# Single PSUM banks in the RG and SSD stages of a hybrid decoder layer on one Trainium2 core

## The chip, the core and the metric

The kernel runs on one core of a Trainium2 chip. The core has five engines that work side by side, each through its own instructions in their order: TensorE (PE) multiplies matrices, VectorE (DVE) and ScalarE (ACT) work elementwise, GpSimd (POOL) does some of that and issues transfers, SyncE (SP) issues transfers. TensorE writes its results to PSUM, which here is used as eight banks of 512 fp32 columns for each of the 128 partitions; VectorE and ScalarE read them there. Everything else lies in SBUF, and transfers (DMA) bring data from and to the memory outside. Engines wait for one another by semaphores.

The metric is the time of one execution in microseconds of device time. An interval or a difference of about 0.2% can be told from noise when several runs are made.

## The reference

One layer of a decoder for 512 prompt tokens and 32 sample tokens, 544 in all, with model width 1024, in fp32:

```python
def layer(x, pos, rg_h0, rg_buf, ssd_h0, ssd_buf, p):
    x = x + 0.5 * rmsnorm(swiglu(rmsnorm(x, p['n_ffn1_pre']), ...), p['n_ffn1_post'])
    mix, new = mixer(rmsnorm(x, p['n_mix_pre']), pos, rg_h0, rg_buf, ssd_h0, ssd_buf, p)
    x = x + rmsnorm(mix, p['n_mix_post'])
    x = x + 0.5 * rmsnorm(swiglu(rmsnorm(x, p['n_ffn2_pre']), ...), p['n_ffn2_post'])
    return x, new

def mixer(u, pos, rg_h0, rg_buf, ssd_h0, ssd_buf, p):
    proj = u @ p['w_in']
    rg_x, rg_g, z, xbc, dt_raw, g_rg, g_ssd = jnp.split(proj, cuts, axis=-1)
    rg_xc, rg_buf_new = causal_conv(rg_x, rg_buf, p['rg_conv_w'], p['rg_conv_b'])
    h, rg_h_new = rg_lru(rg_xc, pos, rg_h0, ...)
    y_rg = h * jax.nn.gelu(rg_g)
    xbc_c, ssd_buf_new = causal_conv(xbc, ssd_buf, p['ssd_conv_w'], p['ssd_conv_b'])
    xs, Bs, Cs = jnp.split(jax.nn.silu(xbc_c), ...)
    y, ssd_h_new = ssd_scan(xh, dt, A, Bs, Cs, ssd_h0)
    y = (y + p['ssd_d'][:, None] * xh) * jax.nn.silu(z)
    y_ssd = y * lax.rsqrt(jnp.mean(y * y, per group) + EPS) * p['ssd_norm_w']
    m = (jax.nn.sigmoid(g_rg) * (y_rg @ p['w_proj_rg'])
         + jax.nn.sigmoid(g_ssd) * (y_ssd @ p['w_proj_ssd']))
    return m @ p['w_out'], new
```

`ssd_scan` goes through each of 8 groups of 4 heads in chunks of 128 tokens, with a state from chunk to chunk; the 8 sample sequences of 4 tokens start from stored states.

## The kernel before

The activations stand transposed: features on partitions, the 544 tokens along the free dimension, in two halves of TH = 272. Every fp32 operand of a large product is split into a high and a low part (`xh`, `xl`; `wh`, `wl`), and a product is the sum of high x high, low x high and high x low, in a fast fp32 format. A **unit** is one 128-column block of weights against all tokens: 8 feature blocks k x 3 passes x 2 halves = 48 matmuls of 128 x 272. `W.get()` hands out the next split weight block and lets later ones be loaded (SP) and split (ScalarE L80, VectorE L83), four blocks deep.

The order of TensorE's instructions is the program's order. On the other engines a scheduler orders them by priority, by default that of the program; `urgent()` raises it, weight splits have a lower one.

PSUM is one pool with three kinds of tiles: `acc`, two slots of two banks each, for the large products; `ps`, two slots of one bank, for small products and transposes; `py`, one slot of two banks. A slot is given to the next tile in turn, and that tile's first write waits until the earlier tile in it was read for the last time.

`gemm` (L289) multiplies both halves in turn, k by k, so that the two banks of an `acc` tile are complete at the same time; `unit` calls it. `unit2` (L338) multiplies two weight blocks together with k outermost, so that the operand blocks are released one after the other during the product. `gemm_half` (L327) takes one half alone; the feed-forward stages and the first products of the mixer use it.

In the **RG and SSD stages** the units of `w_in` run in the order of `specs`: the RG inputs and gates in pairs (`rg_inputs`, `rg_gates`), the merge gates (`gate_units`: Tanh on ScalarE, then a transfer to `th_dram`), and for each group g of 8 four convolution inputs (`conv_in`, into a buffer `cb` from `conv_buf`, of which there are 6), for some g two merge gates, and two z units (Tanh and a copy on ScalarE, a product on VectorE, into one of 4 buffers `z`). `t_ahead` counts the buffers `cb` and `z` in use and runs background steps until one is free.

**Background steps** (`bg`) are generators with the small work: `rg_steps`, `conv_steps`, `group_steps`. After every 4th matmul (5th from the last gates on) `ptick` runs one step, so that small products stand between the large ones in TensorE's order. `group_steps` of a group runs `A(c)` for the four chunks (one `ps` tile: L1063 the product C x B, L1065 three transposes; VectorE L1073, L1078 and ScalarE L1081 read it), `Bs(c)` (L1104, L1106 into `py`, L1108 into `ps`), and for the sample tokens `s1` (L1154), `s2` (L1187, two `ps` tiles of transposed states, copied by ScalarE at L1190), `s3` (L1203, L1210) and `s4`. The order on TensorE is A(0), A(1), s1, Bs(0), A(2), s2, s2, Bs(1), A(3), s3 and so on, with 4 to 15 large matmuls between them. Between A and A of two groups some 65 us pass. `scale_state` on GpSimd prepares the state for the next `Bs`.

Then the **projections**: `projected` loads the 8 blocks of `y_rg` (later of `y_ssd`) with `load_split` (SP; ScalarE L251 for `xh`, VectorE L252 for `xl`, in the place of the operands before), multiplies six units and one `unit2`, and each result is merged with its gate by VectorE (L1390; L1393 and L1394). The background steps of the last two groups still run beside them. After `drain()` the second half of the SSD projection follows, whose first unit takes a `py` tile.

Of the kernel before, what the change touches and what calls it, by code (L numbers as in the profile page):

```python
# [18 lines left out]
P = 128  # L19
D = 1024  # L20
KD = 8
# [82 lines left out]
def hybrid_layer_kernel(  # L104
# [21 lines left out]
    psum = ctx.enter_context(tc.tile_pool(name="psum", bufs=1, space=PSUM))  # L126

    def acc_tile():
        return psum.tile([P, 2, 512], F32, tag="acc", name="acc", bufs=2)

    def ps_tile():
        return psum.tile([P, 512], F32, tag="ps", name="ps", bufs=2)

    def py_tile():
        return psum.tile([P, 2, 512], F32, tag="py", name="py", bufs=1)
# [194 lines left out]
    def unit2(kt, rh, rl):  # L330

        wb = [W.get(), W.get()]
        accs = [acc_tile(), acc_tile()]
        for k in range(kt):
            for j in range(2):
                for i, (w, r) in enumerate(((wb[j][0], rh), (wb[j][0], rl), (wb[j][1], rh))):
                    for h in range(2):
                        PE.matmul(accs[j][:, h, :TH], w[:, k, :], r[k][:, HALF[h]],  # L338
                                  start=(k == 0 and i == 0), stop=(k == kt - 1 and i == 2))
                        ptick()  # L340
        return accs
# [256 lines left out]
    banks = []  # L598
    for t in (acc_tile(), acc_tile()):
        banks += [t[:, 0, :], t[:, 1, :]]  # L600
    banks += [ps_tile(), ps_tile()]
    t = py_tile()
    banks += [t[:, 0, :], t[:, 1, :]]
    for k in range(KD):
        to_half(banks[k], [x for x, n in first], [n for x, n in first], k)
    turned = []
    for k in range(KD):
        turned.append(evac_half(banks[k][:, :TH], 0, k))
# [707 lines left out]
    def gate_units(qs, accs=None):  # L1316
        for q in qs:
            for i in range(2):
                acc = accs[i] if accs else unit(KD, xh, xl)
                th = mt([P, T], "th", 2)  # L1320
                S.activation(two(th), acc[:, :, :TH], AF.Tanh, scale=0.5)
                dma(th_dram[2 * q + i], th)
# [5 lines left out]
    S.activation(two(dt_), adt[:32, :, :TH], AF.Identity, bias=dtc[:, 0:1])  # L1328
    bg.append(rg_steps(2, bufs[2:], gsb[2:]))
# [8 lines left out]
    for g in range(8):  # L1338
        out = {}
        for i, f in enumerate((16 + g, 24 + g, 2 * g, 2 * g + 1)):  # L1340
            acc = unit(KD, xh, xl)
# [7 lines left out]
        for i in range(4, 6):  # L1349
            acc = unit(KD, xh, xl)  # L1350
            out[i] = t_ahead("z", NZ)[:, :T]
# [9 lines left out]
    gate_units(GATES_SSD[7][-1:], unit2(KD, xh, xl))  # L1361
# [14 lines left out]
    def projected(src):  # L1376

        ops = [load_split(src[k], k) for k in range(KD)]
        oh, ol = [a[0] for a in ops], [a[1] for a in ops]
        for n in range(KD):  # L1380
            if n < 6:
                acc = unit(KD, oh, ol)
            else:
                if n == 6:
                    accs = unit2(KD, oh, ol)
                acc = accs[n - 6]
            yield n, acc

    for n, acc in projected(yr_dram):
        V.scalar_tensor_tensor(two(yb[:, n, :]), two(gate(n)), 1.0, acc[:, :, :TH], op0=ALU.add, op1=ALU.mult)  # L1390
# [235 lines left out]
```

## Time and profile before

| | us |
|---|---|
| runs (3) | 1742.36, 1743.77, 1746.11 |
| median | 1743.77 |
| the profiled execution | 1742.75 |
| its span, first to last instruction | 1741.0 |
| mean granted TensorE clock | 0.987 of full speed |

The span falls into the first feed-forward stage (to 451 us), first products of the mixer (to 494), RG stage (to some 606), SSD stage with the projections beside its end (to 1213), and then the second half of the SSD projection, the output projection and the second feed-forward stage.

How to read it: a busy time is the union of an engine's instructions; a matmul's end is modelled, and matmuls overlap, so 292 ns for one doesn't mean 292 ns of TensorE. In lists of waits, "PE ps L1063 <- ACT big L1190" says that TensorE's instruction of line 1063, which writes a tile `ps`, stood idle until ScalarE's instruction of line 1190, which writes a tile `big`, was done. In a timeline the first two columns are start and duration in us. PEclk is the share of its full clock that TensorE was granted.

### The profile page before, as it was taken

To read this page: it belongs to the slowest core of one execution; us is meant where nothing else is said; L and a number is where in the kernel's file an instruction comes from. 1 tells how busy PE (TensorE), PEld (TensorE's weight loads), DVE (VectorE), ACT (ScalarE), POOL (GpSimd) and SP (SyncE) were. 2 spreads that over 40 slices of the span, in tenths; PEclk is the share of its full clock that TensorE was granted. 3 is DMA by queue.
4 is the path that set the end of the run, shared out by engine and by line. 5 is a ranking of instruction groups with operands and counts; after the bars stand their busy time and mean duration, and the time that the engine had idled before them with its cause. 6 is when DMAs were issued, how large, how long until landed. Compare 5 with 4: busy or idle time off the path is not lost. (4 is left out here: it accounts for less than half of the span.)

```text
span 1741.0 us, 32086 instructions
## 1 busy us (share of the span) xinstructions
PE 1688.7 (97%) x13479; PEld 1644.9 (94%) x13479; DVE 1002.2 (58%) x1766; ACT 741.4 (43%) x1205; POOL 266.0 (15%) x376
## 2 busy tenths in 40 slices
PE   9999999999999998999999999999999999999997
PEld 7999999999999997998998989989999999999997
DVE  6532333247757578789688787876558322333345
ACT  5323221234568674455445445434246422221233
POOL 0000000000322125335244334230000000000000
PEclk8999999999999998999999999999999999999998
DMA  6213322232543333534453445666333322223231
GB/s 215 97 60 111 97 74 98 87 106 88 185 135 119 94 101 104 164 96 115 141 157 101 134 132 156 213 185 217 130 106 113 116 80 97 97 74 97 85 110 52
DMA packets 205551, 206.21 MB, mean 118 GB/s; under 512 B 10461, under 2 KB 191785, under 8 KB 205150
## 3 DMA queue, kind: packets, MB, share of 16 engines
q1 hardware_dynamic: 196588, 178.49, 32.8%
q0 software_dynamic: 8336, 24.54, 4.3%
q8 instruction: 106, 1.74, 0.4%
q10 hardware_dynamic: 482, 1.12, 0.2%
q14 instruction: 39, 0.32, 0.1%
HBM read 178.43 MB, written 25.69 MB: 117 GB/s over the span
## 5 line engine op out<-in xcount | busy, mean ns | idle before, releaser
L80 ACT CAST wh<-wraw 128x1024 fp32r<-128x1024 f32 (+1 forms) x274 | 283.7, 1037 | 643.0 <-PE acc L289 534.4
L289 PE MATMUL acc<-xh,wh 128*128 128x272 f32 x2576 | 543.6, 292 | 0.1
L289 PE MATMUL acc<-xh,wl 128*128 128x272 f32 x2576 | 540.9, 291 | 0.0
L289 PE MATMUL acc<-xl,wh 128*128 128x272 f32 x2576 | 538.4, 290 | 0.0
L83 DVE TENSOR_TENSOR wl<-wraw,wh 128x1024 fp32r<-128x1024 f32 (+1 forms) x274 | 331.4, 1212 | 318.3 <-ACT wh L80 315.2
L289 PEld LDWEIGHTS acc<-xh,wh 128*128 128x128 f32 x2576 | 408.3, 190 | 3.6 <-issue 1.4
L289 PEld LDWEIGHTS acc<-xh,wl 128*128 128x128 f32 x2576 | 406.4, 190 | 2.6 <-issue 1.2
L289 PEld LDWEIGHTS acc<-xl,wh 128*128 128x128 f32 x2576 | 407.5, 189 | 1.2 <-issue 0.4
L327 PE MATMUL acc<-xh,wh 128*128 128x272 f32 x384 | 114.9, 299 | 0.0
L327 PE MATMUL acc<-xl,wh 128*128 128x272 f32 x384 | 112.1, 292 | 0.0
L327 PE MATMUL acc<-xh,wl 128*128 128x272 f32 x384 | 111.1, 293 | 0.0
L395 DVE TENSOR_TENSOR gate<-gate,acc 128x544 f32<-128x544 f32 x36 | 26.0, 721 | 130.1 <-PE acc L289 130.1
L887 DVE SCALAR_TENSOR_TENSOR cv<-cb,hp,cv 128x568 f32<-128x568 f32 x96 | 93.9, 978 | 1.1
L289 PE MATMUL acc<-hh,wh 128*128 128x272 f32 x448 | 92.5, 288 | 0.0
L289 PE MATMUL acc<-hl,wh 128*128 128x272 f32 x448 | 92.2, 287 | 0.0
L289 PE MATMUL acc<-hh,wl 128*128 128x272 f32 x448 | 92.2, 288 | 0.0
L1576 POOL TENSOR_TENSOR xtok<-xtok,yo 32x512 f32<-32x512 f32 x1 | 1.3, 1256 | 537.8 <-ACT yo L1575 537.8
L747 POOL MEMSET cb<- 128x3 f32 x40 | 4.2, 104 | 505.9 <-PE acc L327 430.9
L327 PE MATMUL acc<-hh,wh 128*128 128x272 f32 x256 | 75.3, 294 | 2.4 <-DVE yb L451 2.4
L327 PE MATMUL acc<-hl,wh 128*128 128x272 f32 x256 | 74.3, 290 | 0.2
L327 PEld LDWEIGHTS acc<-xh,wh 128*128 128x128 f32 x384 | 73.4, 191 | 1.0
L327 PE MATMUL acc<-hh,wl 128*128 128x272 f32 x256 | 74.1, 290 | 0.0
(399 smaller groups left out, 2646.2 us busy)
## 6 DMA issues: line engine op xcount, KB each, us to landing
wraw<-in_w_in_dram SPq DMA_DIRECT2D x34, 1024.0 KB, 5.8
wraw<-in_ffn_wu_dram SPq DMA_DIRECT2D x24, 1024.0 KB, 5.6
wraw<-in_ffn_wg_dram SPq DMA_DIRECT2D x23, 1024.0 KB, 5.1
wraw<-in_ffn_wd_dram SPq DMA_DIRECT2D x20, 1024.0 KB, 5.2
wraw<-in_w_in_dram SPq DMA_DIRECT2D x18, 512.0 KB, 4.2
big<-acs_dram SPq DMA_DIRECT2D x32, 256.0 KB, 5.5
big<-in_state_ssd_dram SPq DMA_DIRECT2D x32, 256.0 KB, 6.0
out_dram<-big POOLq DMA_DIRECT2D x32, 256.0 KB, 3.5
```

Source lines behind the costliest of these rows:

```text
L80: c = nc.scalar.copy(h[:, :kt], src)
L83: nc.vector.tensor_sub(l[:, :kt], src, h[:, :kt].bitcast(F32))
L289: PE.matmul(acc[:, h, :TH], w[:, k, :], r[k][:, HALF[h]], start=(k == 0 and i == 0), stop=(k == kt - 1 and i == 2))
L327: PE.matmul(acc[:, j, :TH], wb[w][:, k, :], r[k][:, HALF[h]], start=(n == 0), stop=(n == len(order) - 1))
L395: V.tensor_mul(two(gs[j]), two(gs[j]), acc[:, :, :TH])
L747: G.memset(buf[:, 0:3], 0.0)
L887: V.scalar_tensor_tensor(o[:, :CO], buf[:, k:k + CO], ws[k], o[:, :CO], op0=ALU.mult, op1=ALU.add)
L1576: G.tensor_add(x[:n, cs], x[:n, cs], o[:n])
```

## The change

From the merge gates of the RG stage to the end of the first half of the SSD projection, PSUM is divided otherwise: `acc` is three slots of one bank, `ps` three slots of one bank, `py` as before. A class `Banks` closes the pool and opens it anew at `banks.open(True)` and, after the `drain()` of the projections, at `banks.open(False)`; a tile of the new pool waits for the readers of the earlier tiles in its bank.

`halves` takes the place of `unit` there: the first half of the tokens is multiplied through all k into one bank and handed to `out`, then the second half into the next bank. `unit2` takes three `acc` banks and one `ps` bank. Evacuations that took both halves in one instruction (gates, RG gates, z, the merges) take two. `conv_buf`, `t_ahead` and the load of a gate tile come ahead of the products whose results go there.

```diff
     def acc_tile():
-        return psum.tile([P, 2, 512], F32, tag="acc", name="acc", bufs=2)
+        assert not banks.single
+        return banks.pool.tile([P, 2, 512], F32, tag="acc", name="acc", bufs=2)
+
+    def bank_tile():
+        assert banks.single
+        return banks.pool.tile([P, 512], F32, tag="acc", name="acc", bufs=3)
 
     def ps_tile():
-        return psum.tile([P, 512], F32, tag="ps", name="ps", bufs=2)
+        return banks.pool.tile([P, 512], F32, tag="ps", name="ps", bufs=3 if banks.single else 2)
...
+    def halves(out):
+        wb = W.get()
+        for h in range(2):
+            a = bank_tile()
+            for k in range(KD):
+                for i, (w, r) in enumerate(((wb[0], xh), (wb[0], xl), (wb[1], xh))):
+                    PE.matmul(a[:, :TH], w[:, k, :], r[k][:, HALF[h]],
+                              start=(k == 0 and i == 0), stop=(k == KD - 1 and i == 2))
+                    ptick()
+            out(a[:, :TH], h)
+
-    def unit2(kt, rh, rl):
+    def unit2(outs):
         wb = [W.get(), W.get()]
-        accs = [acc_tile(), acc_tile()]
-        for k in range(kt):
+        accs = [[bank_tile(), bank_tile()], [bank_tile(), ps_tile()]]
+        for k in range(KD):
             for j in range(2):
...
+        for j in range(2):
+            for h in range(2):
+                outs[j](accs[j][h][:, :TH], h)
...
     def rg_inputs(r):
-        bufs = []
-        for j in range(2):
-            acc = unit(KD, xh, xl)
-            bufs.append(rg_buf(r + j))
-            for h in range(2):
-                conv_in(bufs[j], acc[:, h, :TH], h)
+        bufs = [rg_buf(r), None]
+        halves(lambda a, h: conv_in(bufs[0], a, h))
+        bufs[1] = rg_buf(r + 1)
+        halves(lambda a, h: conv_in(bufs[1], a, h))
         return bufs
...
             g = t_ahead("z", NZ)[:, :T]
-            S.copy(two(g), acc[:, :, :TH])
+            halves(lambda a, h: S.copy(g[:, HALF[h]], a))
...
+    def gate_out(n):
+        th = mt([P, T], "th", 2)
+        def out(a, h):
+            S.activation(th[:, HALF[h]], a, AF.Tanh, scale=0.5)
+            if h == 1:
+                dma(th_dram[n], th)
+        return out
...
+    banks.open(True)
     bg.append(rg_steps(2, bufs[2:], gsb[2:]))
...
         for i, f in enumerate((16 + g, 24 + g, 2 * g, 2 * g + 1)):
-            acc = unit(KD, xh, xl)
             buf = conv_buf(...)
-            for h in range(2):
-                conv_in(buf, acc[:, h, :TH], h)
+            halves(lambda a, h: conv_in(buf, a, h))
...
-            S.activation(two(out[i]), acc[:, :, :TH], AF.Tanh, scale=0.5)
-            S.copy(two(zr), acc[:, :, :TH])
+            def gated(a, h):
+                S.activation(z[:, HALF[h]], a, AF.Tanh, scale=0.5)
+                S.copy(zr[:, HALF[h]], a)
+            halves(gated)
...
+    def projected(src, out_of):
+        for k in range(KD):
+            xh[k], xl[k] = load_split(src[k], k)
+        for n in range(KD - 2):
+            halves(out_of(n))
+        unit2([out_of(n) for n in range(KD - 2, KD)])
+
+    def rg_out(n):
+        t = gate(n)
+        def out(a, h):
+            cs = HALF[h]
+            V.scalar_tensor_tensor(yb[:, n, cs], t[:, cs], 1.0, a, op0=ALU.add, op1=ALU.mult)
+        return out
...
+    projected(yr_dram, rg_out)
+    projected(ys_dram[:KD], ssd_out)
     drain()
+    banks.open(False)
```

`ssd_out` is like `rg_out`, with the product into the gate tile and, after the second half, the addition to `yb`. The rest of the diff gives other names to local lists called `banks`.

More of the change, by code (lines that the diff above doesn't have):

```diff
@@ L125, in hybrid_layer_kernel, with __init__, open, close @@
     dram = ctx.enter_context(tc.tile_pool(name="dram", bufs=1, space=DRAM))
-    psum = ctx.enter_context(tc.tile_pool(name="psum", bufs=1, space=PSUM))
-    def acc_tile():
-        return psum.tile([P, 2, 512], F32, tag="acc", name="acc", bufs=2)
+    class Banks:
+        def __init__(self):
+            self.stack = None
+            self.open(False)
+        def open(self, single):
+            if self.stack is not None:
+                self.stack.close()
+            self.single = single
+            self.stack = ExitStack()
+            self.pool = pool_of(self.stack, "psum", space=PSUM)
+        def close(self):
+            self.stack.close()
+    banks = Banks()
+    def acc_tile():
+        assert not banks.single
[3 more added lines that the diff above has]
+        return banks.pool.tile([P, 512], F32, tag="acc", name="acc", bufs=3)
     def ps_tile():
-        return psum.tile([P, 512], F32, tag="ps", name="ps", bufs=2)
+        return banks.pool.tile([P, 512], F32, tag="ps", name="ps", bufs=3 if banks.single else 2)
     def py_tile():
-        return psum.tile([P, 2, 512], F32, tag="py", name="py", bufs=1)
+        return banks.pool.tile([P, 2, 512], F32, tag="py", name="py", bufs=1)
     FCH = (6, 8, 8)
@@ L1309, in rg_gates, with gate_units @@
         for j in range(2):
-            acc = unit(KD, xh, xl)
             g = t_ahead("z", NZ)[:, :T]
-            S.copy(two(g), acc[:, :, :TH])
+            halves(lambda a, h: S.copy(g[:, HALF[h]], a))
             gsb.append(g)
         return gsb
-    def gate_units(qs, accs=None):
+    def gate_out(n):
[5 more added lines that the diff above has]
+        return out
+    def gate_units(qs):
         for q in qs:
             for i in range(2):
[L1319 to L1322, printed above, removed]
+                halves(gate_out(2 * q + i))
     set_pace(4)
@@ L1349, in hybrid_layer_kernel @@
         for i in range(4, 6):
-            acc = unit(KD, xh, xl)
-            out[i] = t_ahead("z", NZ)[:, :T]
+            z = out[i] = t_ahead("z", NZ)[:, :T]
             zr = mt([P, T], "th", 2)
-            S.activation(two(out[i]), acc[:, :, :TH], AF.Tanh, scale=0.5)
-            S.copy(two(zr), acc[:, :, :TH])
+            def gated(a, h):
+                S.activation(z[:, HALF[h]], a, AF.Tanh, scale=0.5)
+                S.copy(zr[:, HALF[h]], a)
+            halves(gated)
             V.scalar_tensor_tensor(out[i], out[i], 1.0, zr, op0=ALU.add, op1=ALU.mult)
@@ L1360, in hybrid_layer_kernel @@
     gate_units(GATES_SSD[7][:-1])
-    gate_units(GATES_SSD[7][-1:], unit2(KD, xh, xl))
+    unit2([gate_out(2 * GATES_SSD[7][-1] + i) for i in range(2)])
     def load_split(src, k):
@@ L1374, in gate, with ssd_out, out @@
         return t
[L1376 to L1390, printed above, removed]
-    for n, acc in projected(ys_dram[:KD]):
-        t = gate(8 + n)
-        V.scalar_tensor_tensor(two(t), two(t), 1.0, acc[:, :, :TH], op0=ALU.add, op1=ALU.mult)
-        V.tensor_add(yb[:, n, :], yb[:, n, :], t)
+    def projected(src, out_of):
[10 more added lines that the diff above has]
+        return out
+    def ssd_out(n):
+        t = gate(8 + n)
+        def out(a, h):
+            cs = HALF[h]
+            V.scalar_tensor_tensor(t[:, cs], t[:, cs], 1.0, a, op0=ALU.add, op1=ALU.mult)
+            if h == 1:
+                V.tensor_add(yb[:, n, :], yb[:, n, :], t)
+        return out
+    projected(yr_dram, rg_out)
+    projected(ys_dram[:KD], ssd_out)
     drain()
+    banks.open(False)
     ops = [load_split(ys_dram[8 + k], k) for k in range(KD)]
@@ L1586, in hybrid_layer_kernel @@
     drain()
+    banks.close()
     px.close()
```

26 lines of the change are left out of this document (12 added, 14 removed).

## The prediction

> **What bounds the kernel now.** I read the page first, then TensorE's waits, then the timeline around the longest of them. Of the page:
>
> ```profile
> span 1741.0 us, 32086 instructions
> PE 1688.7 (97%) x13479; PEld 1644.9 (94%) x13479; DVE 1002.2 (58%) x1766; ACT 741.4 (43%) x1205; POOL 266.0 (15%) x376
> ...
> L289 PE MATMUL acc<-xh,wh 128*128 128x272 f32 x2576 | 543.6, 292 | 0.1
> ```
>
> TensorE is the bound: 97% of the span. What can be gained is the time in which it waits. The last row says that the products of `gemm` idle 0.1 us in all, so the accumulators cost nothing today. The waits of TensorE between 640 and 1180 us, the SSD stage (what waited, for whom, us in total, times, longest):
>
> ```profile
> PE ps L1063 <- ACT big L1190: 8.9, 6, 2.2
> PE ps L1065 <- DVE in L1032: 7.0, 2, 5.2
> PE ps L1187 <- ACT small L1081: 3.8, 3, 2.6
> PE ps L1063 <- DVE small L1166: 2.3, 4, 0.9
> PE acc L338 <- DVE yb L1390: 1.5, 1, 1.5
> PE ps L1154 <- ACT cq L899: 0.7, 1, 0.7
> ```
>
> L1063 is the first product of `A`, L1187 the transposes of `s2`, L1154 those of `s1`. None of them needs the result of the instruction that it waits for: they wait for a `ps` slot that this instruction empties. (L1154's named releaser was done long before; its slot was held by the product two before it.) L1065 is another kind: `x0` and `x1` of the first group are not computed yet. The timeline in group 5 shows the mechanism (start, us, engine, line):
>
> ```profile
> 1002.63 0.59 ACT L1190 COPY big<-ps 128x512 f32<-128x512 f32 x1
> ...
> 1009.24 0.59 ACT L1190 COPY big<-ps 128x512 f32<-128x512 f32 x1
> ...
> 1009.88 0.49 PE L1063 MATMUL ps<-in 128*128 128x128 f32 x2 [2.22 <-ACT big L1190]
> ```
>
> Two slots take turns: the two of `s2`, then that of `Bs`, then `A`. `A` gets the slot of the second `s2`, whose copy ends at 9.24 + 0.59 = 1009.83, and starts at 1009.88. With three slots it would get that of the first `s2`, empty since 1003.22, 6.66 us earlier.
>
> **The change part by part.**
>
> *Third slot for small products: gain 17.9 us.* The four slot rows sum to 8.9 + 3.8 + 2.3 + 0.7 = 15.7 us in 14 waits. Idle time counts from the modelled end of a matmul, 0.29 us after its start (the 292 ns of L289), while the next start was due after 0.125 (321 in 40 us, in the windows below), so each stall loses 0.16 us more than its wait says: 14 x 0.16 = 2.2, together 17.9 us.
>
> *What is late next: 1.5 us come back.* These waits stand where VectorE is full (9.89 us of 10 from 800, in the windows below), and ScalarE waits for it. If evacuation doesn't start earlier when TensorE does, the spare time of the third slot is eaten up by what TensorE gained in that group. The tightest is group 4:
>
> ```profile
> 940.32 0.66 PE L1187 MATMUL ps<-ident,big 128*128 128x128 f32 x4 [2.57 <-ACT small L1081]
> ...
> 946.05 0.49 PE L1063 MATMUL ps<-in 128*128 128x128 f32 x2 [0.88 <-ACT big L1190]
> ...
> 948.30 0.64 PE L1203 MATMUL ps<-big,cz 128*32 128x128 f32 x16
> ```
>
> With three slots L1203 would take the one for which L1063 had waited until 946.05 (that of the second `s2`, three products back), 2.25 us before it. Its group's two stalls here alone are 2.57 + 0.88 + 2 x 0.16 = 3.8 us, so some 1.5 us return if the copies stay where they are, and nothing if they move along. The other groups are looser; I allow 0 to 3.6 and take 1.5.
>
> *The clock: gain 3.4 us.* Stretches of the trace, two of them plain, the others of the SSD stage (us, busy time and count of PE, PEld, DVE, ACT, POOL; then granted clock, DMA share, GB/s):
>
> ```profile
> 300.00:340.00 40.00, 40.00 (x321) 40.00 (x321) 12.74 (x13) 10.07 (x12) 0.00 (x0) 1.00 0.29 93
> 452.00:492.00 40.00, 40.00 (x321) 40.00 (x320) 28.89 (x54) 23.60 (x54) 12.69 (x25) 1.00 0.57 175
> 800.00:810.00 10.00, 8.53 (x68) 7.68 (x67) 9.89 (x25) 5.50 (x15) 6.12 (x7) 1.00 0.34 87
> 813.00:817.00 4.00, 2.07 (x16) 1.84 (x15) 3.28 (x8) 2.46 (x5) 2.73 (x6) 0.96 0.00 0
> 817.00:820.00 3.00, 3.00 (x26) 2.35 (x24) 3.00 (x5) 2.45 (x7) 1.52 (x2) 0.50 0.12 23
> 1011.00:1015.00 4.00, 4.00 (x32) 3.33 (x31) 4.00 (x7) 1.42 (x3) 2.62 (x2) 0.57 0.79 256
> 845.00:910.00 65.00, 63.00 (x536) 59.65 (x535) 54.39 (x110) 33.22 (x64) 25.08 (x35) 1.00 0.42 123
> ```
>
> Right after the two stalls of over 2 us that end at 816 and 1010 the clock is halved: 0.57 over 4 us means 3.4 us at one half, which lose 1.7 us. Two such stretches are 3.4 us. Group 4's longer stall (2.57 us) was followed by none, so I keep 0 to 3.4.
>
> *The big products: nothing.* As many matmuls, as many weight loads; only their order changes, from both halves in turn to one half at a time. `gemm_half` (L327) does the latter already: 321 in 40 us at 452, and `gemm` (L289) 321 in 40 us at 300. That is 0.125 us each way.
>
> *Accumulators: nothing.* A half takes 24 x 0.125 = 3.0 us and its bank is wanted two halves later; a pair of banks was wanted one unit of 48 later. Both leave 6 us to empty it, and a half is emptied by less work.
>
> *More, shorter evacuations: hidden.* Per instruction (line, busy us, mean ns):
>
> ```profile
> L1321 ACT ACTIVATE th<-acc 128x544 f32<-128x544 f32 x16 | 9.9, 617 | 0.0
> ...
> L781 ACT COPY z<-acc 128x272 f32<-128x272 f32 x8 | 2.7, 385 | 4.6 <-PE acc L327 4.6
> ```
>
> ScalarE gets 16 more for the gates, 4 for `rg_gates`, 32 for z: 52 x (2 x 385 - 617) = 8.0 us over some 600 us in which it is half idle; VectorE's 16 more at the same 0.15 would be an estimated 2.4. TensorE covers both while banks are freed within 6 us; uncovered, the 8.0 us would be the price. The Trainium skill (Perfetto Trace Analysis, Optimizing Scalar/DVE Operations) puts the fixed overhead of a ScalarE instruction on PSUM at about 51 ns; by that figure it would be an estimated 2.7 us, and the rows, three times as dear, decide.
>
> *Entry to the projections: cost 3.8 us.* In `projected` the first unit uses operand k after 6k matmuls; as halves, after 3k, in half the time. Before it, `load_split` can only fill `xh[7]`, `xl[7]` once the last product has used the old ones, and VectorE is late:
>
> ```profile
> 1097.02 0.42 PE L289 MATMUL acc<-xh,wh 128*128 128x272 f32 x2
> ...
> 1098.26 0.71 DVE L252 TENSOR_TENSOR xl<-in,xh 128x544 fp32r<-128x544 f32 x1
> ...
> 1159.71 0.41 PE L289 MATMUL acc<-xh,wh 128*128 128x272 f32 x2
> ...
> 1160.07 1.78 DVE L252 TENSOR_TENSOR xl<-in,xh 128x544 fp32r<-128x544 f32 x2
> ```
>
> First entry: the 25th product of the first unit starts at 1097.02, so the 22nd, which wants k = 7, comes near 1096.7; `xl[7]` is there at 1098.97: 2.2 us. Second entry: the 19th product starts at 1159.71, when k = 6 is wanted; both splits end at 1161.85, the first near 1160.8, and k = 7 is due 0.4 us after it: 1.6 us. Sum 3.8; from nothing, if VectorE takes the splits sooner, to 7.2, if each wait also brings a 1.7 us clock stretch.
>
> *Reopening the pool: cost 0.7 us.* `banks.open` runs twice, and tiles land on other banks. The first time these have long been empty. The second time the `py` of the next unit takes banks 0 and 1, which by the order of turns hold output 6 of the `unit2` just ended; today it starts at once, while the first evacuation begins:
>
> ```profile
> 1212.64 0.42 PE L289 MATMUL py<-xh,wh 128*128 128x272 f32 x2
> 1212.65 0.71 DVE L1393 SCALAR_TENSOR_TENSOR th<-th,acc 128x544 f32<-128x544 f32 x1
> ```
>
> By the 0.71 of the row for 544 columns two halves are an estimated 0.9 us, of which some 0.2 can start before the end: 0.7, between 0 and 2.3 (if all of output 6 and 7, and the addition of 0.7, go first).
>
> *Steps that move: nothing.* `conv_buf` and `t_ahead` come before the products. Counted through the pace of the background steps, this forces them once, seven steps before the third unit of g = 7: 28 matmuls of cover, 3.5 us, are gone at a place where nothing is awaited soon (the products for the norm of group 5, then a `conv_state`); without that luck it costs up to 3.5 us. Its memset on GpSimd can wait for a buffer longer than today, ahead of `scale_state`, for which the next `Bs` waits:
>
> ```profile
> POOL cb L747 <- DVE cv L887: 62.8, 26, 8.0
> ```
>
> That is 2.4 us each, and no row of today shows TensorE waiting behind it. The load of the gate on SP's queue comes before its unit too, ahead of weights; its slot is freed a unit earlier, so the queue isn't held up. `unit2` holds one of the three small slots for its 12 us, where two have been enough.
>
> **The sum.** The profiled execution took 1742.75 us, 1.75 more than its span; the median of the three runs is 1743.77, 1.0 above it. 1742.75 - 17.9 + 1.5 - 3.4 + 3.8 + 0.7 = 1727.45; on the median, 1728.5. I say **1728**.
>
> **Rivals.**
>
> *VectorE is the bound of the SSD stage (slower).* Place: `A` to `A` of each group, where it is busy 9.89 of 10 us (800 to 810). A third slot then lets TensorE arrive earlier at work that isn't done: the 17.9 and 3.4 us come back as waits for data, the entries and the pool stay: 1742.75 + 3.8 + 0.7 + 1.0 = 1748. It decides from the point where a group needs VectorE for more than the time that remains, 65 - 17.9/8 = 62.8 us. Today (845 to 910) a group takes 54.4 us of 65, 8 us short of that. Against it too: the late half of a group has slack to catch up. Chance 0.06.
>
> *The third slot doesn't serve the waits (slower or no change).* If the tiles don't take turns, or `unit2` and late copies keep one occupied, the slot rows stay: also 1748. For it: nothing but that three slots aren't shown. Against: each wait above ends at the copy two products back. Chance 0.04.
>
> *The clock swings (no change).* If the change of banks every 3 us let TensorE pause often enough, the half clock would come back, say once a group: 8 x 1.7 = 13.6 us on 1728.5, 1742. Against: the stretch at 452 changes banks so, at 40.00 us busy of 40 and clock 1.00. The Trainium skill has this as a rule (TensorE: Matmul & The Clock Gate, A second HAM failure mode: psum-queue depth-cycling): cycling through PSUM banks makes the array idle briefly between groups until its clock oscillates. By that rule, 1742; this trace, with no idle between units, doesn't bear it out. Chance 0.04.
>
> *The dear entry (faster).* 3.6 us return, the entries cost 7.2, no clock stretch goes: 1742.75 - 17.9 + 3.6 + 7.2 + 0.7 + 1.0 = 1737. Chance 0.11, of which 0.02 end within 0.2%.
>
> **How the numbers follow.** The forecast has 0.75. Its low end: nothing returns, entries and pool free, and the 1.5 us of `unit2`'s own waits go too: 1743.8 - 17.9 - 3.4 - 1.5 = 1721, and some 3 for stalls under 0.2 us that the view hides: 1718. Upwards the dear entry, with the 3.5 us of lost cover on top, reaches 1741. What can be told from no change is 0.2%, 3.5 us: 1740.3 to 1747.3. Faster 0.75 + 0.09 = 0.84; same 0.04 + 0.02 = 0.06; slower 0.06 + 0.04 = 0.10. The range 1718 to 1741 leaves out the slower cases and the clock.
>
> **What would show it.** Right: the rows of L1063 on L1190 and L1166, and of L1187 and L1154, shrink from 15.7 us to under 3; clock 1.00 in the SSD stage after its first group; the first two units of the projections wait for `xl` (VectorE's split), some 2 us each; L1065 on L1032 stays at about 7. Wrong: new waits of `Bs`, `s3` or L1065 on VectorE of like size (first rival); slot rows of old size (second); clock under 1 without long stalls (third); accumulator waits in `halves`, which would say that 6 us aren't enough.

## The result and the profile after

The changed kernel takes 1731.04 us (median; 1729.30 to 1733.39) against 1743.07 for the kernel before in the same comparison (1741.53 to 1746.11): a ratio of 0.9929, 95% interval 0.9915 to 0.9943, some 12 us less. The prediction had said 1728, between 1718 and 1741. The profiled execution took 1733.39 us, the slowest of the four, with a mean granted clock of 0.991.

Of the page of the changed kernel, the span, the busy times and one group of large products (count, busy us, mean ns, idle before):

```profile
span 1731.7 us, 32174 instructions
PE 1689.8 (98%) x13479; PEld 1647.2 (95%) x13479; DVE 1001.4 (58%) x1782; ACT 747.7 (43%) x1258; POOL 266.4 (15%) x376
...
L362 PE MATMUL acc<-xh,wh 128*128 128x272 f32 x1312 | 387.5, 295 | 0.9 <-DVE yb L1434 0.5
```

TensorE is the bound as before. L362 is the product of `halves`: it idled 0.9 us in 1312 instructions. ScalarE has 53 instructions more and 6.3 us more to do. Lines of `group_steps` stand 39 further down than before: `A` is L1102 and L1104, the transposes and the copy of `s2` are L1226 and L1229, the two products of `s3` are L1242 and L1249.

The longest waits of TensorE between 640 and 1180 us (what waited, for whom, us in total, times, longest):

```profile
PE ps L1242 <- ACT big L1229: 7.6, 6, 2.6
PE ps L1104 <- DVE in L1071: 7.0, 2, 4.6
PE acc L375 <- ACT th L1397: 0.8, 1, 0.8
PE ps L1249 <- ACT small L1120: 0.8, 2, 0.6
PE ps L1226 <- DVE small L1205: 0.7, 1, 0.7
PE ps L1242 <- DVE small L1154: 0.7, 1, 0.7
...
```

The rows of `A` that waited for a slot (11.2 us before) are gone. Slot waits are now the last three rows shown, 2.2 us in 4 instead of 15.7 in 14, and a part of the first row. That row is new, and it has the same releaser as the costliest of before, the copy of `s2`. The timeline of group 5 shows why (start, us, engine, line):

```profile
1004.49 0.59 ACT L1229 COPY big<-ps 128x512 f32<-128x512 f32 x1 [0.22 <-PE ps L1226]
1005.79 0.60 PE L1226 MATMUL ps<-ident,big 128*128 128x128 f32 x4
1005.94 3.63 DVE L926 SCALAR_TENSOR_TENSOR cv<-cb,hp,cv 128x568 f32<-128x568 f32 x3
...
1007.81 0.43 PE L1242 MATMUL ps<-big,cz 128*32 128x128 f32 x8
1009.60 0.68 ACT L1070 ACTIVATE cv<-cv 128x568 f32<-128x568 f32 x1 [4.53 <-DVE cv L926]
1010.18 0.57 ACT L1229 COPY big<-ps 128x512 f32<-128x512 f32 x1
...
1010.80 0.44 PE L1242 MATMUL ps<-big,cz 128*32 128x128 f32 x4 [2.56 <-ACT big L1229]
```

The second transposes of `s2` end at 1006.39. Their copy stands in ScalarE's order behind a Tanh of the conv, and that Tanh waits 4.53 us for three sums of the conv on VectorE. So the copy starts at 1010.18, 3.8 us after its input, and ScalarE does nothing for 4.53 us of the time. `s3` uses the first `hT` at 1007.81 and then stands until the second is there. Four of the six waits of this row are of this kind, 5.6 us in all, each in the second pair of heads and in the middle of `s3`, at the first product that reads the second `hT`; TensorE comes to `s3(1)` sooner there, since it has no longer stood at `A`. The other two, 2.0 us, stand at the very first product of `s3(0)`, whose `hT` has long been there: they are for the slot of the second `s2`, which the same copy empties. In this first pair (`s2(0)`, `A(3)`, `s3(0)`) it is one and the same copy for which `A` stood before and `s3` stands now, each for a slot.

The Trainium skill (TensorE: Matmul & The Clock Gate, Architectural detail: the array is 16× 32×32, not 1× 128×128) says that ScalarE and VectorE work strictly first in, first out; the 4.53 us of idle ScalarE ahead of a copy agree, for most of which the copy's input was ready.

All waits of TensorE by stage (sums of that view over 540 to 640, 640 to 1075 and 1075 to 1240 us) and the time for which the trace has the clock at one half between 540 and 1240 us:

| kernel | RG: us, times | SSD: us, times | projections: us, times | halved clock, us | median, us | ratio to before, 95% |
|---|---|---|---|---|---|---|
| before | 4.7, 3 | 23.2, 18 | 2.1, 3 | 23.9 | 1743.07 | 1 |
| changed | 0.3, 1 | 15.2, 12 | 3.4, 3 | 20.5 | 1731.04 | 0.9929 (0.9915 to 0.9943) |
| two slots, spare bank | 0.3, 1 | 21.2, 19 | 3.4, 3 | 3.4 | 1734.56 | 0.9951 (0.9935 to 0.9968) |
| s3 later | 0.3, 1 | 12.0, 7 | 0.0, 0 | 13.7 | 1719.84 | 0.9862 (0.9847 to 0.9876) |
| s3 later, two slots | 0.3, 1 | 22.6, 18 | 0.4, 1 | 10.2 | 1734.08 | 0.9947 (0.9928 to 0.9965) |
| order of before's products alone | 4.4, 3 | 23.4, 20 | 3.6, 5 | 13.7 | 1744.61 | 1.0012 (1.0002 to 1.0021) |

The clock differs between executions of one kernel (below), so the profiled runs show where waits are, and the medians what a change is worth. The two profiled spans here differ by only 9.3 us because the changed one lost 2.4 us by its 385th large product, at 80 us, where nothing has been changed yet.

Two places besides the SSD stage moved. In the **RG stage** three waits of before are gone; these are its rows, of the same view between 540 and 640 us:

```profile
PE py L959 <- DVE big L252: 2.2, 1, 2.2
PE ps L869 <- DVE big L863: 1.7, 1, 1.7
PE ps L875 <- DVE small L874: 0.8, 1, 0.8
```

Of the changed kernel one row of 0.3 us is left there. In **group 7** a wait is new: the second x tile (L1071) comes late for the first `A`, as the timeline of the changed kernel shows:

```profile
1110.23 0.27 PE L1104 MATMUL ps<-ident,in 128*128 128x128 f32 x1
...
1111.09 1.22 DVE L83 TENSOR_TENSOR wl<-wraw,wh 128x1024 fp32r<-128x1024 f32 x1
1112.23 0.68 DVE L1071 SCALAR_TENSOR_TENSOR in<-cv 128x512 f32<-128x512 f32 x1
...
1112.97 0.69 PE L1104 MATMUL ps<-ident,in 128*128 128x128 f32 x2 [2.47 <-DVE in L1071]
```

### The profile page after: what moved, and what is told of

Its sections match the earlier page's. It is cut to its first block, busy times and chain, and to the rows that moved or that the text cites. A ratio compares the mean times of both kernels' runs of the same rounds, so it can differ in the third digit from the quotient of the medians.

```text
span 1731.7 us, 32174 instructions
## 1 busy us (share of the span) xinstructions
PE 1689.8 (98%) x13479; PEld 1647.2 (95%) x13479; DVE 1001.4 (58%) x1782; ACT 747.7 (43%) x1258; POOL 266.4 (15%) x376
## 5 line engine op out<-in xcount | busy, mean ns | idle before, releaser
L362 PE MATMUL acc<-xh,wh 128*128 128x272 f32 x1312 | 387.5, 295 | 0.9 <-DVE yb L1434 0.5
L362 PE MATMUL acc<-xl,wh 128*128 128x272 f32 x1312 | 386.8, 295 | 0.0
L362 PE MATMUL acc<-xh,wl 128*128 128x272 f32 x1312 | 386.6, 295 | 0.0
L313 PE MATMUL acc<-xh,wh 128*128 128x272 f32 x1264 | 261.8, 288 | 0.0
L313 PE MATMUL acc<-xh,wl 128*128 128x272 f32 x1264 | 261.5, 288 | 0.0
L313 PE MATMUL acc<-xl,wh 128*128 128x272 f32 x1264 | 261.0, 288 | 0.0
L362 PEld LDWEIGHTS acc<-xh,wh 128*128 128x128 f32 x1312 | 250.5, 191 | 3.7 <-issue 1.2
L362 PEld LDWEIGHTS acc<-xl,wh 128*128 128x128 f32 x1312 | 250.8, 191 | 2.4 <-issue 1.0
L362 PEld LDWEIGHTS acc<-xh,wl 128*128 128x128 f32 x1312 | 250.6, 191 | 2.0 <-issue 0.8
L313 PEld LDWEIGHTS acc<-xl,wh 128*128 128x128 f32 x1264 | 198.9, 189 | 0.0
L313 PEld LDWEIGHTS acc<-xh,wh 128*128 128x128 f32 x1264 | 198.6, 189 | 0.0
L313 PEld LDWEIGHTS acc<-xh,wl 128*128 128x128 f32 x1264 | 197.7, 189 | 0.0
L351 PE MATMUL acc<-xh,wh 128*128 128x272 f32 x384 | 115.6, 301 | 0.0
L351 PE MATMUL acc<-xl,wh 128*128 128x272 f32 x384 | 112.7, 294 | 0.0
L351 PE MATMUL acc<-xh,wl 128*128 128x272 f32 x384 | 111.4, 293 | 0.0
L313 PE MATMUL acc<-hh,wh 128*128 128x272 f32 x448 | 92.5, 288 | 0.0
L313 PE MATMUL acc<-hl,wh 128*128 128x272 f32 x448 | 92.3, 288 | 0.0
L313 PE MATMUL acc<-hh,wl 128*128 128x272 f32 x448 | 92.2, 288 | 0.0
```

What stands on the lines that cost most here:

```text
L313: PE.matmul(acc[:, h, :TH], w[:, k, :], r[k][:, HALF[h]], start=(k == 0 and i == 0), stop=(k == kt - 1 and i == 2))
L351: PE.matmul(acc[:, j, :TH], wb[w][:, k, :], r[k][:, HALF[h]], start=(n == 0), stop=(n == len(order) - 1))
L362: PE.matmul(a[:, :TH], w[:, k, :], r[k][:, HALF[h]], start=(k == 0 and i == 0), stop=(k == KD - 1 and i == 2))
```

## The experiments

**Two slots, the bank given to the accumulators.** Which part made the gain, the third slot or the single banks?

```diff
-... tag="acc", name="acc", bufs=3)
+... tag="acc", name="acc", bufs=4)
...
-... tag="ps", name="ps", bufs=3 if banks.single else 2)
+... tag="ps", name="ps", bufs=2)
...
-        accs = [[bank_tile(), bank_tile()], [bank_tile(), ps_tile()]]
+        accs = [[bank_tile(), bank_tile()], [bank_tile(), bank_tile()]]
```

> The changed kernel with the two slots of before: its small products get 2 slots instead of 3, and the bank left over becomes a fourth accumulator bank (unit2 then holds all four). TensorE's order of instructions stays as in the changed kernel. If the third slot made the gain (my theory): TensorE waits again for the slot of the second s2's copy (A on big, s2 on small), 10 to 18 us in the SSD stage where the changed kernel shows about 1.4 us of slot waits, and the time is 1739 to 1746. If the halves made it (a bank at a time, evacuated after 24 products): the time stays at 1729 to 1733. A mean of both, 1735, would say that each gave a part; the gain of the RG stage (6.9 us to the first A of group 0) should then stay, as no slot row of before stood there beyond 3.6 us.

1739.33 us, ratio 0.9977 (0.9965 to 0.9988). The slot waits came back, but so did a cost of another kind. This is the whole list of waits between 1195 and 1215 us, where the pool is opened again:

```profile
PE py L313 <- DVE th L1442: 2.6, 1, 2.6
```

With four accumulator banks in turn, the first tile after the reopening lands on a bank that is emptied last. The run with a spare bank takes that out:

```diff
-... tag="ps", name="ps", bufs=3 if banks.single else 2)
+... tag="ps", name="ps", bufs=2)
+
+    def spare_tile():
+        return banks.pool.tile([P, 512], F32, tag="spare", name="spare", bufs=1)
...
-        accs = [[bank_tile(), bank_tile()], [bank_tile(), ps_tile()]]
+        accs = [[bank_tile(), bank_tile()], [bank_tile(), spare_tile()]]
```

> The changed kernel with two slots again, but the bank left over is used by unit2 alone (one spare tile), so that the three accumulator banks turn as in the changed kernel. The run with four accumulator banks waited 2.9 us at 1204 for the first tile after the pool's reopening, with 3.4 us of halved clock behind it (4.1 us in all), which the changed kernel doesn't. If that wait came from which banks unit2 held last: it falls below 0.5 us here, and the time is 1733.5 to 1737: the third slot by itself is then worth only some 4 us of the 12. If it comes from the slots: the wait stays, 1738 to 1742, and the third slot is worth 8.

1734.56 us. The wait at the reopening is gone, and the slot waits are back, here the longest between 640 and 1180 us (its lines stand 3 further down; L1105 is `A`, L1229 `s2`, L1232 its copy):

```profile
...
PE ps L1105 <- ACT big L1232: 5.9, 4, 2.0
PE ps L1105 <- DVE small L1208: 2.8, 2, 2.3
PE ps L1229 <- ACT small L1123: 2.8, 5, 1.4
PE ps L1105 <- DVE small L1157: 1.6, 1, 1.6
...
```

So the third slot removes the waits that the prediction names, and yet it is worth only 3.5 us by the medians (by the intervals from nothing to 7), while single banks with two slots already gain 8.5.

**s3 later.** If the data wait took the place of the slot wait, more distance between copy and use must pay.

```diff
+        yield from wait(3)
         yield from s3(0)
...
+        yield from wait(3)
         yield from s3(1)
...
             last_tanh[0] = rstd_act(v[:, :, :TH], two(sqs[0]), two(r))
-        yield from wait(3)
...
-        yield from wait(3)
```

> The changed kernel, with three background steps (12 products, 1.5 us) more ahead of each s3, and the two stretches of three steps that end a group left out, so that a group has as many steps. My theory: what is left of the stalls in the SSD stage is s3's first product waiting for the copy of the second s2 that ScalarE makes late (7.6 us in 6 waits, and three stretches of halved clock behind the two longest, some 5 us). 1.5 us more cover takes 6 waits to at most 2 of 1 us: 7.6 falls to 1 to 2.5 us, halved clock at 884 and 1010 goes, time 1719 to 1725. Rival: ScalarE and VectorE set the pace and the waits move to the next consumer (Bs(3), s4, the norm's product v, or the next group's A) with the same sum: 1729 to 1734.

1719.84 us, 11.2 below the changed kernel. The longest waits between 640 and 1180 us:

```profile
PE ps L1104 <- DVE in L1071: 4.6, 1, 4.6
PE py L1325 <- DVE big L1320: 3.5, 1, 3.5
PE ps L1242 <- ACT big L1229: 2.4, 2, 1.5
...
```

The wait of `s3` fell from 7.6 to 2.4 us. Group 7 lost its wait for x too. One new wait came, that of the norm's product in group 5 (3.5 us). The test of the other half is the same edit with two slots and the spare bank:

> s3 three steps later, with two slots and a spare bank. With s3 where the change has it, the third slot was worth 3.5 us (1734.6 against 1731.0), though 15 us of slot waits come back without it: my theory is that the data wait of s3 took the place of the slot wait of A, both for the same late copy. So with s3 later the third slot must be worth much more: slot waits of 12 to 18 us stay here (A still waits for the second s2's copy), s3 waits for less than 1 us, and the time is 1730 to 1737, 10 us or more above the 1719.8 of three slots. Rival: later s3 is a gain of its own that doesn't need the third slot; then 1721 to 1726.

1734.08 us: without the third slot, later `s3` gains nothing (0.5 us), with it 11.2; the slot gains 3.5 without later `s3`, and 14.2 with it. Its rows:

```profile
PE ps L1105 <- ACT big L1232: 4.7, 4, 1.9
...
PE ps L1229 <- ACT small L1123: 3.7, 3, 1.6
...
PE ps L1105 <- DVE small L1208: 2.4, 4, 1.1
```

The wait of `A` and that of `s3` stand one behind the other, both for late copies of `s2`: taking away one alone hands most of its time to the other.

**The late copy on VectorE.**

```diff
-                    S.copy(t, pp.rearrange("p (b n) -> p b n", b=4))
+                    (S.copy, V.tensor_copy)[i](t, pp.rearrange("p (b n) -> p b n", b=4))
```

> The changed kernel, with the copy of the second s2 of each pair on VectorE instead of ScalarE (16 copies of 128x512). My theory: that copy is late because it stands in ScalarE's order behind a tanh of the conv which itself waits for VectorE, not because ScalarE is full; on VectorE it stands behind no such wait. s3's wait for it falls from 7.6 us to below 2, the halved clock at 884 and 1010 goes, and the time is 1717 to 1724. Rival: VectorE is the engine that is late in these stretches (9.9 us busy of 10); then 16 x 0.6 = 10 us more work there delays x tiles and cbm, waits for VectorE (in, small) grow by 4 to 10 us, and the time is 1731 to 1738.

1735.30 us, 4.3 more than the changed kernel: the theory's numbers failed. The wait of `s3` doubled:

```profile
PE ps L1242 <- DVE big L1229: 14.9, 10, 2.7
```

In VectorE's timeline of group 5 the copy stands behind the very sums for which ScalarE's Tanh had waited:

```profile
1010.13 3.62 DVE L926 SCALAR_TENSOR_TENSOR cv<-cb,hp,cv 128x568 f32<-128x568 f32 x3
1013.67 0.68 DVE L1229 COPY big<-ps 128x512 f32<-128x512 f32 x1
```

So the root is VectorE's conv work, and on either of these engines the copy is queued behind it. What helped is distance, not the other engine.

**The buffers of group 7 taken late.** What forces seven background steps ahead is undone, for two units only (with `late`, `halves` hands out both halves at its end):

```diff
...
+            late = g == 7 and i >= 2
+            bs = [] if late else [conv_buf(st)]
+            def taken(a, h):
+                if not bs:
+                    bs.append(conv_buf(st))
+                conv_in(bs[0], a, h)
-            halves(lambda a, h: conv_in(buf, a, h))
+            halves(taken, late)
...
```

> The changed kernel, but in group 7 the third and fourth conv unit take their buffer after both halves are done, as before the change; nothing else moves. This takes away the seven background steps that are forced ahead of the third unit there. My theory: in the changed kernel they bring A(0) of group 7 28 products (3.5 us) nearer to the second x tile, which VectorE finishes late, and cost the wait of 2.5 us on it at 1110 us plus half of the 3.4 us of halved clock behind it. So that wait falls below 0.5 us, no halved clock at 1110 to 1117, and the time is 4 us below the changed kernel's: ratio to before 0.9905, 1727. Rival: the x tile is late because VectorE's splits for the projections now go ahead of it; then the wait stays at 1.5 to 3 us whatever the steps do, or the splits become late instead and the entry to the projections waits 1 to 4 us, and the time is 1730 to 1733.

1727.17 us, ratio 0.9908 (0.9893 to 0.9923), 3.9 below the changed kernel, as expected in size. But the rival was right in part: the wait for x went, and the entries to the projections wait. Between 1060 and 1180 us:

```profile
PE acc L362 <- DVE xl L276: 2.1, 3, 1.1
PE acc L381 <- DVE yb L1448: 1.6, 1, 1.6
```

So undoing the forced steps traded the wait of 2.5 us, and the halved clock behind it, for an entry cost of 2.1. All waits of TensorE between 540 and 1240 us fell only from 18.9 to 17.7, and by the two intervals the 3.9 us lie between nothing and 7; whether it is worth that much isn't shown, as a run below says too.

**What shortened the RG stage.** First, both halves evacuated together:

```diff
-            out(a[:, :TH], h)
+            if h == 0:
+                a0 = a
+        out(a0[:, :TH], 0)
+        out(a[:, :TH], 1)
```

> The changed kernel with its three slots and three accumulator banks, but a half's evacuation is issued only when both halves of its tile are done, as before the change (TensorE's order stays). The run with two slots still lost 8 us less than before between the first A of group 0 and that of group 7, and its RG stage was as short as the changed kernel's. If that part comes from the first half being evacuated 24 products (3 us) earlier, which brings conv's work to VectorE sooner: the wait for x in group 0 grows from 4.6 us to about 7, the RG stage's waits for VectorE come back, and the time is 1735 to 1740. If it comes from something else (the order of the halves, buffers taken ahead of the products): 1729 to 1733. Third: banks are then freed late, accumulator waits appear in halves (0.3 us or more in many units): over 1740.

1729.34 us, ratio 0.9918 (0.9904 to 0.9933), no different from the changed kernel. But the edit didn't do what it was to do. ScalarE's timeline near 570 us, first of the kernel before, where the first two rows are the copies of a unit's first and second half into its conv buffer:

```profile
570.46 0.36 ACT L756 COPY cb<-acc 128x272 f32<-128x272 f32 x1
570.73 0.34 ACT L758 COPY cb<-acc 128x240 f32<-128x240 f32 x1
```

and then of this run, the same two copies:

```profile
565.61 0.39 ACT L798 COPY cb<-acc 128x272 f32<-128x272 f32 x1 [0.50 <-PE acc L362]
...
570.84 0.34 ACT L800 COPY cb<-acc 128x240 f32<-128x240 f32 x1
```

The program issues them together, and still the first runs 5.2 us ahead: with a bank of its own it needs only its own half, and the scheduler orders ScalarE's instructions anew. Over the 34 conv units of the RG and SSD stages the first copy starts a median of 5.3 us before the second in the changed kernel and in this one, 0.27 us in the kernel before. So this run left the early copy in, and says nothing about it. The next one also takes all buffers after the products:

```diff
-        bufs = [rg_buf(r), None]
-        halves(lambda a, h: conv_in(bufs[0], a, h))
+            def taken(a, h):
+                if h == 0:
+                    bufs.append(rg_buf(r + j))
+                conv_in(bufs[j], a, h)
+            halves(taken)
```

and likewise for the gates, the SSD units and the z tiles.

> As the run in which both halves are evacuated together, and every buffer (conv buffers, gate and z tiles) is also taken only after the products, as before the change. What stays of the change: the order of the products, single banks, the third slot. The RG stage between 540 and 640 us was 7 us shorter in every changed kernel so far (stalls of 1.7, 0.8 and 2.2 us for VectorE and 6.8 us of halved clock gone), with two slots too and with late evacuation. If taking the buffers ahead did that: these waits come back, and the time is 1733 to 1739. If the order of the products did it (or where the schedule then happens to put the weight split on VectorE): they stay away. In SSD no step is forced ahead any more, so the wait for x at the first A of group 7 (2.5 us) goes, and 1 to 4 us come back at the entries to the projections, as in the run with late buffers in group 7: 1725 to 1730.

1730.00 us, ratio 0.9922 (0.9901 to 0.9943). The three waits stay away (0.3 us between 540 and 640), so it isn't the place of the buffers. The entries wait 2.1 us as in the run with late buffers, and the wait for x in group 7 is gone as there; but against 1729.34 of the run before it, which had that wait, this gained nothing. Then the order of the products alone, in the kernel before, with pairs of banks:

```diff
-        for k in range(kt):
-            for i, (w, r) in enumerate(...):
-                for h in range(2):
...
+        turn = [(k, i, h) for k in range(kt) for i in range(3) for h in range(2)]
+        if apart[0]:
+            turn.sort(key=lambda t: t[2])
+        for k, i, h in turn:
...
```

> The kernel before with one thing of the change alone: from the RG stage to the end of the second projection, unit's products run one half of the tokens after the other. Pairs of banks, two slots, joint evacuation and the place of the buffers stay. So far two slots with everything else of the change are 8.5 us faster than before (1734.6), and neither early evacuation nor buffers taken ahead explain it. If the order of the products does: the RG stage is 7 us shorter (waits of 1.7, 0.8 and 2.2 us for VectorE gone, no halved clock at 574 and 618), slot waits in the SSD stage stay at 12 to 17 us, and the time is 1733 to 1737. If single banks are needed for it: the three waits stay, 1741 to 1746 (up to 4 more if the entries to the projections wait).

> The kernel before with that order of the products in the RG stage alone (its inputs, gates and gate units); the SSD stage and the projections as before. If the order removes the three waits of the RG stage by itself: 1735 to 1738, and the SSD stage keeps its slot waits of about 15.7 us and its halved clock. If the gain of the order lies in the SSD stage: 1740 to 1745.

1744.61 us (ratio 1.0012, 1.0002 to 1.0021) with that order through the projections, 1744.14 (1.0004, 0.9992 to 1.0017) in the RG stage alone. The waits between 540 and 640 us of the first:

```profile
PE py L963 <- DVE big L252: 2.1, 1, 2.1
PE ps L873 <- DVE big L867: 1.5, 1, 1.5
PE ps L879 <- DVE small L878: 0.8, 1, 0.8
```

They are the three of before. In pairs the first copy starts only 0.28 us ahead of the second, although its half is done 3 us earlier. So the order alone gains nothing, and what is gained needs a bank for each half. Every run with single banks has the early copy and lacks the three waits, every run with pairs is the other way round. That the early copy is the cause is the reading that fits all of them; forcing it late with single banks was not tried, so it isn't shown.

The traces show one more thing that goes with the banks: the order on VectorE just ahead of the first of the three waits, here of the kernel before,

```profile
570.62 1.20 DVE L83 TENSOR_TENSOR wl<-wraw,wh 128x1024 fp32r<-128x1024 f32 x1
571.75 0.71 DVE L863 TENSOR_TENSOR big<-big 32x544 f32<-32x544 f32 x1
```

and of the changed kernel:

```profile
571.16 0.70 DVE L902 TENSOR_TENSOR big<-big 32x544 f32<-32x544 f32 x1
...
572.65 1.23 DVE L83 TENSOR_TENSOR wl<-wraw,wh 128x1024 fp32r<-128x1024 f32 x1
```

L863 and L902 are the same instruction, for which TensorE stood 1.7 us in the kernel before. A weight split of 1.20 us goes ahead of it in the three runs with pairs, and behind it in all eleven with single banks. So most of this wait goes with an order that the scheduler chose. Whether it chose it because of the early copies, or only happened to, is open.

**More lead for group 0, and for the norm.** Two attempts on what s3 later left over, both with its edit:

```diff
-        yield from wait(5)
+        yield from wait(13 if g == 0 else 5)
         A(0)
```

> The kernel with s3 three steps later, and eight background steps (32 products, 4 us) more ahead of A(0) in group 0 alone. Theory: the wait of 4.6 us for x in group 0 is only the lead time of the first group, nothing else waits there, so it falls below 1 us, the 6.8 us of halved clock behind it go too, and the time is 7 to 8 us below that of s3 later: 1711 to 1714. Rival: the first group is then later for everything behind it (the next group's x, the conv buffers), and the wait is only moved: 1717 to 1722.

1719.59 us, ratio 0.9863 (0.9842 to 0.9885): no change against s3 later. Of the view between 640 and 1180 us:

```profile
...
PE ps L1242 <- ACT big L1229: 3.3, 3, 1.8
PE ps L1226 <- ACT cb L795: 1.6, 1, 1.6
PE ps L1104 <- DVE in L1071: 1.4, 1, 1.4
...
```

The wait for x fell from 4.6 to 1.4 us, but the waits of the whole SSD stage sum to 12.3 us against 12.0: others grew by as much. The rival was right. To this run the next adds:

```diff
         s4()
-        yield from wait(3)
...
         fin()
-        yield from wait(12)
+        yield from wait(15)
```

> As the run before, and the norm's product v comes three steps (1.5 us) later after the work of y that feeds it, by issuing that work three steps earlier, right behind s4. Theory: the wait of 3.5 us of v in group 5 (its squares stand behind the evacuation of a half and a weight cast in ScalarE's order) falls below 2.2 us, halved clock behind it goes, and the time is 3 to 5 us below the run before: 1707 to 1710. Rival: issuing y earlier only puts it ahead of other work on VectorE; x tiles or Bs wait instead: 1711 to 1716.

1725.32 us, ratio 0.9896 (0.9881 to 0.9911), 5.7 worse than the run before. The norm's product still waits 3.1 us, and new waits stand beside it:

```profile
PE ps L1163 <- DVE small L1154: 1.6, 2, 1.4
...
PE py L1145 <- POOL big L1132: 1.4, 1, 1.4
```

The first waits for the running state (L1154 on VectorE), the second for a product of `scale_state` on GpSimd (L1132). That y's work now goes ahead of them would explain it; it wasn't tested.

## Why the prediction was nearly right

The sign and the range held, and the waits that were to go went; the time was 3 us above the forecast. That it came so near is in good part luck: two of its steps were wrong by more than that, in opposite directions. The third slot, for which the sum had 17.9 less 1.5 us, is worth 3.5 us here, and 8.5 of the 12 us came with single banks and two slots, for which it had nothing. Of the signs that were to show it right, the slot rows fell below 3 us and the row of x stayed at 7; but the clock was not whole behind the first group, and the first units of the projections did not wait for `xl`.

*Third slot, 17.9 us:* right as a count of what goes. 13.5 of the 15.7 us of slot waits went (14 waits to 4), with 0.16 us for each of the ten some 15.1 us. The run with two slots and a spare bank has them back.

*What is late next, 1.5 us:* this step failed. It asked only whether a third slot would be free in time. That is what came in two waits, 2.0 us at the first product of `s3(0)`, near the 1.5. But it had no term for the late instruction's result, and `s3` needs that too: its `hT` are these copies, the second of them 12 products on in the second pair. (The copy at 1009.24, in the prediction's own timeline, is such an `hT`.) There 5.6 us came back in four waits. Together it is 7.6 us in 6, with 0.16 each 8.6, where 3.6 was the most allowed. The runs with later `s3`, with three slots and with two, show that the rest of the slot's worth was behind it.

*The clock, 3.4 us:* mis-sized. In the SSD stage the profiled runs have 17.1 us at one half before and after, though the stalls are fewer. Stretches of the changed kernel right behind its stalls of 2.6 and 2.5 us (us, busy time and count of PE, PEld, DVE, ACT, POOL; granted clock):

```profile
1010.00:1017.00 7.00, 6.20 (x32) 5.72 (x33) 3.97 (x9) 2.51 (x6) 0.64 (x1) 0.52 0.41 120
1113.00:1116.00 3.00, 3.00 (x14) 3.00 (x15) 0.97 (x4) 0.27 (x1) 1.54 (x2) 0.50 0.86 272
```

*Big products, accumulators, evacuations, nothing:* "hidden" held for the cost. The accumulators' waits are short (0.8 us at `unit2`, 0.9 in all units of `halves`). ScalarE got 6.3 us more, the prediction's estimate was 8.0; a half takes 383 ns where the pair took 609, so splitting costs 157 ns:

```profile
L1397 ACT COPY th<-acc 128x272 f32<-128x272 f32 x32 | 12.2, 383 | 0.0
```

The estimate from the Trainium skill's 51 ns (Perfetto Trace Analysis, Optimizing Scalar/DVE Operations), 2.7 us, was too small by more than half. But "nothing" missed the gain that came with single banks. In the RG stage 4.4 us of waits went, and the 6.8 us of halved clock there, 3.4 more; in group 0 the waits for x fell from 7.0 us in two to 4.6 in one. By the reading above, which isn't shown, it is because a bank for each half lets ScalarE start sooner: over the 34 conv units a first copy starts a median of 1.0 us after the end of the unit's last product in the kernel before, and 3.2 us ahead of it in the changed one. The prediction counted an early evacuation only as a bank freed sooner, not as work that starts sooner on a full engine. The Trainium skill (Perfetto Trace Analysis, Optimizing Tensor Performance, Matmuls) says that independent groups should rotate through different banks so that one's evacuation overlaps the next one's products; the 8.5 us of single banks with two slots fit that.

*Entry to the projections, 3.8 us:* 0 in the changed kernel, whose splits were done before they were wanted, since the forced steps had moved the small work ahead. Where these are undone it is 2.1 us in 3 waits: right in kind, half in size.

*Steps that move, nothing:* failed. The prediction saw the seven forced steps and priced their lost cover at up to 3.5 us, but took the place to be one where nothing is awaited. All later steps move up with them: the first `A` of group 6 comes 28 products earlier in TensorE's order than before, that of group 7 35 (a step takes five by then), and there it meets an x tile that isn't ready: 2.5 us, and 3.4 us of halved clock behind it. Undoing it gave 3.9 us by the medians in one run and nothing in another, so what the step cost in all stays open.

*Reopening the pool, 0.7 us:* no wait of 0.2 us or more stands there. The run with four accumulator banks shows the other case, 2.6 us, just above the bound of 2.3.

*The row of x at about 7 us:* the sum stayed at 7.0, but by chance: 4.6 in group 0, and 2.5 new in group 7.

Together, each stall at 0.16 us more than its wait and halved clock at half its length: 15.1 (slots), 2.6 (x in group 0), 8.1 (RG) and 1.2 (accumulators and L1108, 2.6 us in 5 waits before, 1.7 in 3 now) gained, 8.6 (`s3`) and 4.4 (group 7) lost, net 14.0. The profiled spans differ by 9.3 after 2.4 lost at the start, 11.7. Some 2 us aren't accounted for.

*The rivals:* the first came in part. Slot waits did come back as waits for data that VectorE makes late, but 5.6 us of them and not 17.9, so it did not set the pace of the whole stage. The third slot serves its waits. Between 130 and 1500 us the clock never halved without a stall in front, so the rule on cycling through banks isn't borne out. The dear entry did not come.

## What to carry to other kernels

Where a wait for a buffer goes, look for the next use of the late instruction's *result*, not only for the next use of a buffer: the two stand in series, and the worth of either edit (here 3.5 and 0.5 us alone, 14.7 together) shows only when both are made. A step that is forced ahead moves everything behind it in its queue; find the tightest wait behind, not the nearest. An accumulator of its own for each part let the evacuation start with the part here (3.2 us ahead of the unit's end), which a pair did not, even with the products in the right order.

## What the hardware showed

The clock halves for 3.41 us or two or three times that, and whether it does so after a stall of 2 to 3 us can't be told from its length. In the fourteen traces, between 130 and 1500 us, 37 starts of matmuls came 2 to 3 us after the one before (three others, just ahead of a longer stall, left out); 20 of these were followed by a halved stretch within 5 us, or had it begin in the stall. The same stall of 2.74 us at the first `A` of group 7 was followed by one in the changed kernel, and by none in four others. All 12 stalls of over 4.8 us had one, of four between 3.4 and 3.8 us three. By 1.7 us for each 3.41, the 23.9 and the 3.4 us of the table's extremes differ by some 10 us. Runs of one kernel differ so too: of the kernel before, beside the last run above, one of 1738.87 us had a mean granted clock of 0.993, one of 1745.51 had 0.987. The Trainium skill (TensorE: Matmul & The Clock Gate, Part 1: The HAM clock gate) has a free-running window of 3413 ns, which the steps and the uneven outcome agree with; its limit of about 3.4 us of idle before the clock drops is longer than what is seen here.
